# A shorter lead for the weight halves during attention, with attention and the modulation loads moved later

## The chip, the core and the metric

The kernel runs on one core of one Trainium2 chip. The time is the device time of one execution in microseconds (us), as the median of several executions. The profile is one more execution, taken with the hardware profiler; its times within the program are counted from the first instruction ("the span").

TensorE is called PE in the profile (PEld is its loading of weights), VectorE DVE, ScalarE ACT, GpSimd POOL and SyncE SP. SP issues nearly all loads from HBM; its rows are marked SPq.

## The reference

One layer of a transformer variant on 256 tokens of width 1024, in float32: a token mixer with two branches, then a feed-forward part with a short convolution. All of it is modulated by six vectors that come from a condition vector `c`.

```python
mod = silu(c) @ w_ada + b_ada                 # 1024 -> 6 x 1024: sh1, sc1, g1, sh2, sc2, g2
h = x * (1 + sc1) + sh1
proj = h @ w_in                               # 1024 -> mq mk mv (512 each) rq rk (512) rv rg (1024) g_a g_r (1024)
y_a = attention(rope(mq), rope(mk), mv)       # 8 heads of 64, causal (256 tokens make one block)
y_r = retention(rot(rq), rot(rk), rv)         # 4 heads, keys of 128, values of 256, decay mask
y_r = silu(rg) * head_norm(y_r)
merged = sigmoid(g_a) * (y_a @ w_proj_moba) + sigmoid(g_r) * (y_r @ w_proj_ret)
x = layer_norm(ALPHA * x + g1 * (merged @ w_out))
h = x * (1 + sc2) + sh2
g, u = h @ w_ff_gate, h @ w_ff_up             # 1024 -> 2816
y = (gelu(conv3(g)) * u) @ w_ff_down
out = layer_norm(ALPHA * x + g2 * y)
```

## The kernel before

**Products in three parts.** Each float32 operand is split into a high part of a reduced format (`whi`, a copy by ACT) and the rest (`wlo`, a subtraction by DVE: raw minus high). A product is then three matmuls: high by high, high by low, low by high (`mm3`, lines L115 to L117).

**Weight tiles and halves.** Weights come from HBM as raw tiles of 128 x 2048 float32, 1 MB each, into four rotating buffers (`RAW_BUFS = 4`). A raw tile has two halves of 128 x 1024; each half gets one `whi` (line L1261, ACT) and one `wlo` (line L1275, DVE), and eight pairs of these can be alive (`HL_BUFS = 8`). This text numbers weight tiles from 0 at the start of the main stream: tile n holds halves 2n and 2n+1.

**Steps.** After the opening part A (the first modulation vectors, and the first 1024 columns of `w_in` with parts of `g_a`), the program is a list of steps, one for each half. Step s multiplies half s: in the mixer these are 12 matmuls of 128x512. The mixer's steps are, with the two banks of PSUM that they write:

| steps | weights | banks | who reads the banks afterwards |
|---|---|---|---|
| 0 to 3 | rk | 0, 1 | ACT (L485) |
| 4 to 7, 8 to 11 | rv | 2, 3, then 0, 1 | ACT (L493) |
| 12 to 15, 16 to 19 | rg | 2, 3, then 0, 1 | ACT (L501), DVE (L502) |
| 20, 21 and 22, 23 | rest of g_a | 2, 3, then 0, 1 | DVE (L510) |
| 24 to 27, 28 to 31 | g_r | 2, 3, then 0, 1 | ACT (L518) |
| 32, 33 and 34, 35 | w_proj_moba | 2, 3, then 0, 1 | DVE (L525) |
| 36 to 39, 40 to 43 | w_proj_ret | 2, 3, then 0, 1 | DVE (L544) |

A group of steps can't start before the banks it writes have been read out by the engine in the last column, for the group two rows of banks earlier. Steps 44 to 51 are `w_out` and the first layer norm, later ones the feed-forward part.

**What sets the order.** Nothing is rescheduled: each engine executes its instructions in the order in which the program writes them. The loop over the steps writes, for step s: first the side work of two places in the step, and between these the preparation of weight halves (`prep_to`) up to half s plus a lead of `LOOKAHEAD = 6`; then the step's matmuls and what reads out its banks; then the side work of a third place. `prep_halves` writes the high copy of one half further than the subtraction that it is at. So ACT meets the high copy of half s + 7 before the read-out of step s, and whatever that copy waits for, the read-out behind it waits for too.

**Side work** is written as generators that go on at each of the three places. `mixers` is attention: `rope` of the two token halves of q and k (DVE), 16 transposes (`rot_T`, PE line L993), then for 8 heads scores (PE, L1046), the mask with the row maximum (DVE, L1055), the exponential and its scaling (ACT, L1082 and L1078), transposes (PE, L1093) and the product with v (`attend`, PE line L1069). It also ropes rq and rk, and at `i == 10` it starts `retention`, whose first product with the decay mask is DVE line L1157. Its 16 transposes of the result are PE line L1196, and the splits of these are ACT line L92 and DVE line L93.

**Modulation units.** The rest of `w_ada` (sections 2 to 5) comes as units: raw tiles of 1 MB in the same four buffers, placed in the stream of loads behind given weight tiles (`extra`). Each unit is two multiply-and-sum instructions on DVE (line L227, `junk<-raw,srow`, one for each half), of which one is written behind the subtraction of each weight half as long as a unit has arrived. Section 4 is g1, needed at the end of step 47; sections 2 and 3 are needed at the first layer norm.

**Loads.** SP issues the loads in the order of the stream. A load goes into the buffer of the load four places earlier in the stream, and waits in SP's queue until DVE has done with that tile: for a weight tile, the subtraction of its second half; for a unit, its second L227.

Of the kernel before, what the change touches and what calls it, by code (L numbers as in the profile page):

```python
# [17 lines left out]
EPS = 1e-5  # L18
ALPHA = 2.0 ** 0.25
RROPE, RROT, TL = 5, (8, 10), 4  # L20
LOOKAHEAD = 6
RAW_BUFS = 4
HL_BUFS = 8
NG = 4
ROT_AT, RV_AT, RG_AT, LN1_AT = 3, 12, 20, 48


CONST_AT, FIRST = 1, 1
# [32 lines left out]
def _body(nc, a, out, pe, act, dve, sp, cst, wts, big, tmp, ps, dram):  # L61
# [14 lines left out]
    def slot(n, shape, dt=F32):  # L76
        if n in pairs:
            assert pairs[n].dtype == dt
            return pairs[n].rearrange("p e (k t) -> p e k t", k=shape[2])
        if n not in place:  # L80
            return big.tile(shape, dt, tag=f"A{n}", name=f"A{n}")
        pair, e = place[n]
        assert pairs[pair].dtype == dt
        v = pairs[pair][:, e, :math.prod(shape[1:])]
        return v.rearrange("p (a b) -> p a b", a=shape[1]) if len(shape) == 3 else v
# [394 lines left out]
    S = {}  # L480
# [515 lines left out]
                       p.rearrange("p (i t) -> p i t", i=4), AF.Copy)  # L996

    def evac_A():
        v = slot(4, [128, 2, 512])
        for t in range(2):  # L1000
            S["rqk", t] = slot(f"R{t}", [128, 1024])
        for c in range(2):
            for t in range(2):
                o = qk[t][:, c * 512:c * 512 + 512]
                dve.tensor_tensor(o, pa[2 * c + t], o, OP.add)
        for t in range(2):
            act.activation(v[:, t], pa[4 + t], AF.Copy)
        for t in range(2):
            act.activation(S["rqk", t][:, 0:512], pa[6 + t], AF.Copy)
        S["qk"], S["v"] = qk, v  # L1010

    def mixers():

# [4 lines left out]
        roped(0)  # L1018
        for i in range(ROT_AT + 2):
            yield  # L1020
            if i == 0:
                roped(1)
            yield
            if i == ROT_AT + 1:
                for w in range(4):
                    rot_T(qk[w // 2], w // 2, qkT, w % 2, 4 + w)
            yield
# [193 lines left out]


    extra = {}
    for sec, at in ((2, (6, 7, 9, 10)), (3, (11, 12, 13, 14)), (4, (16, 18, 19, 20)), (5, (38, 41, 44, 47))):
        for u in range(4):
            done = (lambda sec=sec: rows_done(sec)) if sec > 3 else (lambda: None)
            extra.setdefault(at[u], []).append((a["ada2"][sec - 2, u], ada_unit(sec, u, done)))
# [61 lines left out]
    def prep_to(n, force=False):  # L1289
        while prepped[0] < min(n, 2 * len(main)) and (force or live[0] < HL_BUFS):  # L1290
            next(pg)
# [6 lines left out]
    pg = prep_halves()  # L1298
    prep_to(FIRST)
    evac_A()  # L1300
    prep_to(FIRST + 2)
    sides = [mixers()]

    def run_sides():
# [4 lines left out]
    for s, (need, rel, fn) in enumerate(steps):  # L1309
        S["main"] = s  # L1310
        if s == LN1_AT + 8:
            sides.append(residual())
        run_sides()
        prep_to(max(need) + 1, True)
        late = LN1_AT < s < LN1_AT + 8
        if not late:
            prep_to(max(need) + 1 + (LOOKAHEAD if s < LN1_AT - 1 else HL_BUFS))
        run_sides()
        for e in waiting:
            if e[0] <= s:  # L1320
                e[1]()
        waiting[:] = [e for e in waiting if e[0] > s]
        fn([tiles[h] for h in need])
        for h in rel:
            tiles.pop(h)
            live[0] -= 1
        while s % 2 and later and later[0][0] <= s:
            later.pop(0)[1]()
        run_sides()
        if late and s >= LN1_AT + PRIME:  # L1330
            if s == LN1_AT + PRIME:
                next(pg)
            elif s > LN1_AT + 4:
                prep_to(max(need) + 1 + HL_BUFS)
# [96 lines left out]
```

## Time and profile before

| what | value |
|---|---|
| median of 3 executions | 426.39 us (426.08 to 426.46) |
| the profiled execution's own time | 427.17 us |
| its span | 425.4 us |
| granted TensorE clock, mean | 0.995 |
| busy: PE / DVE / ACT / POOL | 97% / 87% / 58% / 3% of the span |
| moved by DMA | 105.58 MB, 248 GB/s on average |
| step 0 of the main stream starts on PE | 63.47 us |
| step 18 starts | 129.26 us |
| step 36 starts | 186.68 us |

How to read it: PE's durations are modelled and overlap (a 128x512 matmul is shown with 0.39 us, and the next one starts 0.227 us later), so where PE stood still is read from the starts of its rows. DVE's and ACT's rows overlap a little too; the price of an instruction in a queue is the distance from its start to the next start. In a row of the timeline the first number is the start, the second the duration, and a bracket tells how long the engine was idle before and what ended that.

### The profile page before, as it was taken

What the parts mean: (1) busy time and instruction counts of PE and PEld (TensorE: products, weight loads), DVE (VectorE), ACT (ScalarE), POOL (GpSimd) and SP (SyncE); (2) the same over time, 40 slices, a digit from 0 to 9 for tenths busy, and PEclk for the clock granted to TensorE, in tenths of its full rate; (3) what the DMA queues carried; (4) which work ended last, traced back from release to release, by engine and by line L of the source; (5) the groups of instructions that cost most, each with busy time, mean ns of one, the idle gap of its engine ahead of it and who ended that gap; (6) DMA issues with size and microseconds to landing.
All of it is one profiled execution on the core that took longest, in us unless ns stands there. A gap on an engine that the chain in (4) does not pass through costs nothing.

```text
span 425.4 us, 5803 instructions
## 1 busy us (share of the span) xinstructions
PE 413.5 (97%) x2104; PEld 347.5 (82%) x2104; DVE 370.2 (87%) x613; ACT 245.5 (58%) x397; POOL 14.0 (3%) x26
## 2 busy tenths in 40 slices
PE   7999999999999999999999999999999999999992
PEld 4888887786888888888888898888888888888882
DVE  5979898969998999799777896999999888789876
ACT  4666558759865578524453886655545445455600
POOL 0000000100000000001000001000000010012200
PEclk9999999999999999999999999999999999999997
DMA  8998995886569778689652085985776776540001
GB/s 284 408 410 329 420 416 186 296 346 223 186 277 353 247 296 306 290 324 368 246 197 99 2 309 190 368 300 184 312 245 233 280 282 235 193 186 2 1 25 74
DMA packets 18828, 105.58 MB, mean 248 GB/s; under 512 B 2288, under 2 KB 3568, under 8 KB 8048
## 3 DMA queue, kind: packets, MB, share of 16 engines
q1 hardware_dynamic: 17280, 99.97, 62.7%
q0 software_dynamic: 1376, 4.99, 3.5%
q8 instruction: 16, 0.26, 0.2%
q10 hardware_dynamic: 144, 0.26, 0.2%
q14 instruction: 12, 0.10, 0.1%
HBM read 104.15 MB, written 1.06 MB: 247 GB/s over the span
## 4 chain that ended last, share of the span: by engine, by line
PE 86%; DVE 6%; DMA 3%; ACT 1%; issue 1%; SPq 1%; DVEq 0%; ACTq 0%
PE P L124 16%; PE P L115 14%; PE P L116 14%; PE P L117 14%; PE P L301 13%; PE P L126 8%; DVE wlo L1275 3%; DMA raw<-in_winB 2%; DMA raw<-in_strm 1%; PE P L688 1%; PE P L690 1%; PE P L691 1%; DVE junk L227 1%; PE P L1069 1%; DVE A L1055 1%
## 5 line engine op out<-in xcount | busy, mean ns | idle before, releaser
L1275 DVE TENSOR_TENSOR wlo<-raw,whi 128x1024 fp32r<-128x1024 f32 x118 | 141.9, 1219 | 15.2 <-ACT whi L1261 14.9
L1261 ACT ACTIVATE whi<-raw 128x1024 fp32r<-128x1024 f32 x118 | 122.4, 1057 | 53.8 <-PE P L117 21.0
L115 PE MATMUL P<-whi,AH 128*128 128x512 f32 x160 | 63.5, 397 | 0.6 <-DVE mx L1055 0.6
L116 PE MATMUL P<-wlo,AH 128*128 128x512 f32 x160 | 62.5, 390 | 0.2 <-DVE wlo L1275 0.2
L117 PE MATMUL P<-whi,AH 128*128 128x512 f32 x160 | 62.4, 390 | 0.0
L301 PE MATMUL P<-whi,AH 128*128 128x512 f32 x160 | 42.0, 391 | 1.2 <-DVE AH L267 0.9
L124 PE MATMUL P<-AYa,whi 128*128 128x512 f32 x144 | 39.2, 393 | 0.0
L227 DVE CUSTOM_DVE_ANT_0 junk<-raw,srow 128x1024 bf16<-128x1024 f32 x32 | 38.9, 1217 | 0.0
L124 PE MATMUL P<-AYb,whi 128*128 128x512 f32 x144 | 38.6, 390 | 0.0
L301 PEld LDWEIGHTS P<-whi,AH 128*128 128x128 f32 x160 | 29.8, 188 | 8.8 <-ACT whi L284 2.4
L115 PEld LDWEIGHTS P<-whi,AH 128*128 128x128 f32 x160 | 30.1, 188 | 7.6 <-DVE mx L1055 1.0
L116 PEld LDWEIGHTS P<-wlo,AH 128*128 128x128 f32 x160 | 30.1, 188 | 6.5 <-DVE wlo L1275 0.6
L117 PEld LDWEIGHTS P<-whi,AH 128*128 128x128 f32 x160 | 30.0, 188 | 6.4
L465 ACT ACTIVATE A<-P 128x256 f32<-128x256 f32 x36 | 13.7, 381 | 34.5 <-PE P L126 32.6
L124 PEld LDWEIGHTS P<-AYb,whi 128*128 128x128 f32 x144 | 27.0, 188 | 6.0
L284 ACT ACTIVATE whi<-raw 128x512 fp32r<-128x512 f32 (+1 forms) x26 | 20.8, 824 | 17.8 <-DMA raw<-in_strm 16.6
L287 DVE TENSOR_TENSOR wlo<-raw,whi 128x512 fp32r<-128x512 f32 (+1 forms) x26 | 23.6, 935 | 6.0 <-ACT whi L284 5.9
L124 PEld LDWEIGHTS P<-AYa,whi 128*128 128x128 f32 x144 | 25.1, 190 | 3.6
L126 PEld LDWEIGHTS P<-AYa,wlo 128*128 128x128 f32 x144 | 22.0, 189 | 2.8
L301 PE MATMUL P<-wlo,AH 128*128 128x512 f32 x80 | 23.2, 389 | 0.0
L126 PE MATMUL P<-AYb,wlo 128*128 128x256 f32 x144 | 23.1, 283 | 0.0
L126 PE MATMUL P<-AYa,wlo 128*128 128x256 f32 x144 | 22.9, 282 | 0.0
(302 smaller groups left out, 732.7 us busy)
## 6 DMA issues: line engine op xcount, KB each, us to landing
raw<-in_ada SPq DMA_DIRECT2D x16, 1024.0 KB, 4.9
raw<-in_wup SPq DMA_DIRECT2D x11, 1024.0 KB, 5.5
raw<-in_wgate SPq DMA_DIRECT2D x11, 1024.0 KB, 4.9
raw<-in_wdown SPq DMA_DIRECT2D x11, 1024.0 KB, 5.1
raw<-in_winB SPq DMA_DIRECT2D x10, 1024.0 KB, 7.5
raw<-in_strm SPq DMA_DIRECT2D x8, 1024.0 KB, 7.6
raw<-in_strm SPq DMA_DIRECT2D x12, 512.0 KB, 7.5
raw<-in_winGr SPq DMA_DIRECT2D x4, 1024.0 KB, 6.1
```

The costliest lines, as they stand in the source:

```text
L115: pe.matmul(o, lh, rh, start=start, stop=False)
L116: pe.matmul(o, lh, rl, start=False, stop=False)
L117: pe.matmul(o, ll, rh, start=False, stop=stop)
L124: pe.matmul(o, wh[:, k * 128:(k + 1) * 128], x2[k], start=k == 0, stop=False)
L126: pe.matmul(o[:, :256], wl[:, k * 128:(k + 1) * 128], x2[k][:, 0], start=False, stop=k == n - 1)
L227: dve.tensor_tensor_reduce(out=nobody(j if own else None), in0=raw, in1=srow, scale=1.0, scalar=0.0, op0=OP.mult, op1=OP.add, accum_out=mo ...
L284: act.activation(hi[:, o], raw[:, o], AF.Copy)
L287: dve.tensor_tensor(lo[:, o], raw[:, o], f(hi[:, o]), OP.subtract)
L301: pe.matmul(pa[b0 + c // 512 * 2 + t], x[xi][:, j, t * 128:(t + 1) * 128], ws[k][:, c:c + 512], start=first and (xi, k) == (0, 0), stop=la ...
L465: act.activation(t, p[:, 256:], AF.Copy)
L1261: act.activation(hi, src, AF.Copy)
L1275: dve.tensor_tensor(lo, src, f(hi), OP.subtract)
```

## The change

Five edits.

- While the step is below 22, halves are prepared four ahead of the step and not six (`NEAR`, `NEAR_TO`). From step 22 on it is six as before.
- `evac_A` is cut in two. The four additions on DVE for q and k stay where they were; the four copies on ACT (v, and the first half of rq and rk) become `evac_B`, written behind the preparation of halves 1 to 3; before, they stood ahead of the preparation of halves 1 and 2.
- The rope of the second token half of q and k is written in step 1, not in step 0.
- `ROT_AT` goes from 3 to 4: the transposes of q and k and everything of attention behind them, with the retention that it starts, come one step later.
- The units of sections 2, 3 and 4 move to later places in the stream of loads: section 2 behind weight tiles 9 to 12 (before: 6, 7, 9, 10), section 3 behind 13 to 16 (before: 11 to 14), section 4 behind 17 to 20 (before: 16, 18, 19, 20).

```diff
-LOOKAHEAD = 6
+LOOKAHEAD, NEAR, NEAR_TO = 6, 4, 22
...
-ROT_AT, RV_AT, RG_AT, LN1_AT = 3, 12, 20, 48
+ROT_AT, RV_AT, RG_AT, LN1_AT = 4, 12, 20, 48
...
     def evac_A():
-        v = slot(4, [128, 2, 512])
-        for t in range(2):
-            S["rqk", t] = slot(f"R{t}", [128, 1024])
         for c in range(2):
             for t in range(2):
                 o = qk[t][:, c * 512:c * 512 + 512]
                 dve.tensor_tensor(o, pa[2 * c + t], o, OP.add)
+        S["qk"] = qk
+
+    def evac_B():
+        v = S["v"] = slot(4, [128, 2, 512])
         for t in range(2):
             act.activation(v[:, t], pa[4 + t], AF.Copy)
         for t in range(2):
+            S["rqk", t] = slot(f"R{t}", [128, 1024])
+        for t in range(2):
             act.activation(S["rqk", t][:, 0:512], pa[6 + t], AF.Copy)
-        S["qk"], S["v"] = qk, v
...
         for i in range(ROT_AT + 2):
             yield
-            if i == 0:
+            if i == 1:
                 roped(1)
             yield
             if i == ROT_AT + 1:
...
-    for sec, at in ((2, (6, 7, 9, 10)), (3, (11, 12, 13, 14)), (4, (16, 18, 19, 20)), (5, (38, 41, 44, 47))):
+    for sec, at in ((2, (9, 10, 11, 12)), (3, (13, 14, 15, 16)), (4, (17, 18, 19, 20)), (5, (38, 41, 44, 47))):
...
     prep_to(FIRST)
     evac_A()
-    prep_to(FIRST + 2)
+    prep_to(FIRST + 3)
+    evac_B()
     sides = [mixers()]
...
         if not late:
-            prep_to(max(need) + 1 + (LOOKAHEAD if s < LN1_AT - 1 else HL_BUFS))
+            prep_to(max(need) + 1 + (NEAR if s < NEAR_TO else LOOKAHEAD if s < LN1_AT - 1 else HL_BUFS))
```

**How the instructions move.** First VectorE at the start of the main stream. `wlo` is the subtraction of a weight half, A2a and A2b are the two token halves of q and k, A8a is the rope's scratch tile; the first rows are the additions of `evac_A`. Before:

```order
L1005 TENSOR_TENSOR A2a<-P_132,A2a 128x512
L1005 TENSOR_TENSOR A2b<-P_133,A2b 128x512
L1275 TENSOR_TENSOR wlo<-raw,whi 128x1024 x2
L983 TENSOR_TENSOR A8a<-A2a,tables 128x16x32 x2
L986 TENSOR_TENSOR A2a<-A2a,tables 128x1024
L987 TENSOR_TENSOR A2a<-A2a,A8a 128x1024
L1275 TENSOR_TENSOR wlo<-raw,whi 128x1024 x4
L983 TENSOR_TENSOR A8a<-A2b,tables 128x16x32 x2
L986 TENSOR_TENSOR A2b<-A2b,tables 128x1024
L987 TENSOR_TENSOR A2b<-A2b,A8a 128x1024
L1275 TENSOR_TENSOR wlo<-raw,whi 128x1024 x5
```

Now, the same place:

```order
L1002 TENSOR_TENSOR A2a<-P_132,A2a 128x512
L1002 TENSOR_TENSOR A2b<-P_133,A2b 128x512
L1277 TENSOR_TENSOR wlo<-raw,whi 128x1024 x3
L983 TENSOR_TENSOR A8a<-A2a,tables 128x16x32 x2
L986 TENSOR_TENSOR A2a<-A2a,tables 128x1024
L987 TENSOR_TENSOR A2a<-A2a,A8a 128x1024
L1277 TENSOR_TENSOR wlo<-raw,whi 128x1024 x2
L983 TENSOR_TENSOR A8a<-A2b,tables 128x16x32 x2
L986 TENSOR_TENSOR A2b<-A2b,tables 128x1024
L987 TENSOR_TENSOR A2b<-A2b,A8a 128x1024
L1277 TENSOR_TENSOR wlo<-raw,whi 128x1024 x5
```

Half 3 now stands ahead of the first rope, and two halves stand between the ropes where there were four.

Then SyncE's loads of the main stream: `winB` are weight tiles 0 to 9, `winGa` 10 and 11, `winGr` 12 to 15, `wpm` 16 and 17, `wpr` 18 to 21, and `ada` is a modulation unit. Before, from weight tile 2 on:

```order
L102 DMA raw<-in_winB 128x2048 x5
L102 DMA raw<-in_ada 128x2048
L102 DMA raw<-in_winB 128x2048
L102 DMA raw<-in_ada 128x2048
L102 DMA raw<-in_winB 128x2048 x2
L102 DMA raw<-in_ada 128x2048
L102 DMA raw<-in_winGa 128x2048
```

Now:

```order
L102 DMA raw<-in_winB 128x2048 x8
L102 DMA raw<-in_ada 128x2048
L102 DMA raw<-in_winGa 128x2048
```

Two units have gone from between the weight tiles of the attention steps; they come back further on, one behind weight tile 15 and one behind 17, so that from tile 9 to tile 20 weights and units alternate one by one.

Last, VectorE around halves 32 to 38. `junk` is the multiply-and-sum of a modulation unit, AYa the split of the retention's result, which step 36 multiplies. Before:

```order
L1275 TENSOR_TENSOR wlo<-raw,whi 128x1024 x2
L227 ISA junk,mod<-raw,srow 128x1024
L227 ISA mod 128x1
L1275 TENSOR_TENSOR wlo<-raw,whi 128x1024
L227 ISA junk,mod<-raw,srow 128x1024
L227 ISA mod 128x1
L1275 TENSOR_TENSOR wlo<-raw,whi 128x1024 x3
L227 ISA junk,mod<-raw,srow 128x1024
L227 ISA mod 128x1
L93 TENSOR_TENSOR AYa<-P_1621,AYa 128x4x128
```

Now:

```order
L1277 TENSOR_TENSOR wlo<-raw,whi 128x1024
L227 ISA junk,mod<-raw,srow 128x1024
L227 ISA mod 128x1
L1277 TENSOR_TENSOR wlo<-raw,whi 128x1024
L227 ISA junk,mod<-raw,srow 128x1024
L227 ISA mod 128x1
L1277 TENSOR_TENSOR wlo<-raw,whi 128x1024
L227 ISA junk,mod<-raw,srow 128x1024
L227 ISA mod 128x1
L93 TENSOR_TENSOR AYa<-P_1643,AYa 128x4x128
```

A unit's multiply-and-sum now stands behind every weight half here, where before some halves had none; and the split of the retention's result now stands behind half 38, where it stood behind half 37.

## The prediction

> **What bounds the kernel now.** I first read the span and then TensorE's rows in order of time, looking for places where a matmul starts later than the pitch allows. The profiled execution took 427.17 us in all, 0.78 above the median of 426.39; I work out differences in its span and put them on the median.
>
> ```profile
> span 425.4 us, 5803 instructions
> ```
>
> PE is busy in nearly all of it (97%, in the table above); a change in the order of side work can win only where PE stands still. In the main stream there are four such places, all in steps 3 to 12:
>
> ```profile
> 71.63 0.39 PE L115 MATMUL P<-whi,AH 128*128 128x512 f32 x1
> 72.17 0.50 PE L116 MATMUL P<-wlo,AH 128*128 128x512 f32 x1 [0.15 <-DVE wlo L1275]
> 72.51 0.39 PE L117 MATMUL P<-whi,AH 128*128 128x512 f32 x1
> ...
> 77.63 0.93 PE L993 MATMUL P<-ident,A2a 128*128 128x128 f32 x7
> 79.30 0.55 PE L993 MATMUL P<-ident,A2b 128*128 128x128 f32 x3 [0.75 <-DVE A2b L987]
> ...
> 95.60 1.45 PE L1093 MATMUL P<-ident,A 128*128 128x128 f32 x6
> ...
> 103.84 0.39 PE L117 MATMUL P<-whi,AH 128*128 128x512 f32 x1
> 104.79 0.50 PE L115 MATMUL P<-whi,AH 128*128 128x512 f32 x1 [0.56 <-DVE mx L1055]
> ...
> 118.07 0.82 PE L1093 MATMUL P<-ident,A 128*128 128x128 f32 x6
> ```
>
> Two 128x512 matmuls start 0.227 us apart when nothing stops them. The first stall (half 3's `wlo`, which stands behind the first rope) makes this 0.54, and 0.34 to the next start: 0.42 us. The transposes come at 0.109 us each, so the eight of A2a should have handed over at 78.50 and not 79.30: 0.80 (the second rope is late). Six transposes take 0.82 us undisturbed and took 1.45: 0.63 (scaled exponentials late). Step 12 started 0.95 us after the matmul before it: 0.72 (the mask of heads 6 and 7, which reads the banks that step 12 writes). Sum: 2.57, say **2.6 us**, all there is to win.
>
> Then I read the windows for the engine that would come next.
>
> ```profile
> 90.00:100.00 10.00, 9.80 (x55) 7.54 (x54) 5.93 (x17) 8.66 (x24) 0.00 (x0) 1.00 0.52 186
> 150.00:160.00 10.00, 10.00 (x46) 8.29 (x45) 9.96 (x17) 7.84 (x13) 0.00 (x0) 1.00 0.77 298
> 160.00:170.00 10.00, 10.00 (x46) 8.29 (x45) 10.00 (x15) 8.54 (x13) 0.00 (x0) 1.00 0.89 321
> 180.00:190.00 10.00, 10.00 (x46) 8.29 (x45) 10.00 (x16) 2.77 (x3) 0.00 (x0) 1.00 0.80 288
> ```
>
> The third busy figure is DVE. It is idle 4 us of ten around 95 us, in attention, and full from 150 to 170 and from 180 to 190, with PE never waiting for it there: it lives on the lead that it built up before. The change takes modulation work out of the first stretch and puts it into the second. That is where I look for the price.
>
> **The four stalls, after the change.** The subtractions of halves 1 to 3 now stand ahead of the first rope.
>
> ```profile
> 63.47 0.39 PE L115 MATMUL P<-whi,AH 128*128 128x512 f32 x1
> ...
> 66.03 1.22 DVE L1275 TENSOR_TENSOR wlo<-raw,whi 128x1024 fp32r<-128x1024 f32 x1 [1.41 <-ACT whi L1261]
> 67.18 1.28 DVE L983 TENSOR_TENSOR A8a<-A2a,tables 128x512 f32<-128x512 f32 x2
> ...
> 70.90 4.62 DVE L1275 TENSOR_TENSOR wlo<-raw,whi 128x1024 fp32r<-128x1024 f32 x4
> ...
> 84.85 0.28 DVE L1055 CUSTOM_DVE_ANT_0 A<-P,tables 128x128 f32<-128x128 f32 x1
> 85.59 0.28 DVE L1055 CUSTOM_DVE_ANT_0 A<-P,tables 128x128 f32<-128x128 f32 x1
> ...
> 91.34 1.06 ACT L1261 ACTIVATE whi<-raw 128x1024 fp32r<-128x1024 f32 x1 [4.63 <-DMA raw<-in_winB]
> ```
>
> A rope costs 70.90 - 67.18 = 3.7 us. The wait of 1.41 us goes with `evac_B` behind the high copies, so half 3 is done by about 67, against 71.9 needed; two halves (2.3) and both ropes (7.4) end near 77, and the transposes now stand behind step 5, not before 63.47 + 6 x 2.72 = 79.8. Stalls one and two go. The third goes with the units: in ACT's queue attention's exponentials stood behind the weight copy at 91.34, which waited 4.63 us for its load, and that load came between two unit loads which are now further on. For the fourth, the mask of heads 6 and 7 is written right ahead of step 12, with one step less between. From the second group of scores on, DVE has four masked heads and one subtraction to do, 0.74 (85.59 - 84.85) and 1.14 each, from 0.75 us before step 11 starts, of which the third head must be done when step 12 starts 2.85 later: 3 x 0.75 + 1.14 + 0.1 - 0.75 = 2.74, the 0.1 for a reciprocal. It just fits, if DVE comes to it idle, which it does without units. I take 0; the bounds are 0 and the 0.72 of now. So PE is **2.6 us early at step 18**.
>
> **What the second stretch costs.** Which DVE work must end before PE may go on? Step 36 writes banks 2 and 3, which L525 reads out. So I follow DVE's queue from the retention's first mask product (L1157) to the first half of L525. The product can't come early: it needs PE's scores behind step 18 (17 before).
>
> ```profile
> 128.47 0.38 PE L1155 MATMUL P<-AYa,AYb 128*128 128x128 f32 x2
> 129.26 0.47 PE L115 MATMUL P<-whi,AH 128*128 128x512 f32 x1
> ...
> 127.14 1.22 DVE L1275 TENSOR_TENSOR wlo<-raw,whi 128x1024 fp32r<-128x1024 f32 x1
> 128.28 1.22 DVE L227 CUSTOM_DVE_ANT_0 junk<-raw,srow 128x1024 bf16<-128x1024 f32 x1
> ...
> 129.42 1.02 DVE L1157 TENSOR_TENSOR A<-P,A2a 128x384 f32<-128x384 f32 x2
> ...
> 135.55 1.21 DVE L1157 TENSOR_TENSOR A<-P,A2b 128x384 f32<-128x384 f32 x2 [1.65 <-PE P L1155]
> ...
> 175.95 1.29 DVE L93 TENSOR_TENSOR AYa<-P,AYa 128x512 fp32r<-128x512 f32 x2 [2.87 <-ACT AYa L92]
> ...
> 182.91 1.28 DVE L525 TENSOR_TENSOR A<-P,A 128x512 f32<-128x512 f32 x2
> ```
>
> Before: from 129.42 to the end of L525's first half, 182.91 + 0.6 = 183.5, are 54.1 us, of which 1.65 and 2.87 idle: 49.6 us of work. In it are 16 subtractions (halves 24 to 39) and 12 unit halves (9 to 20, from 0). Now DVE arrives at L1157 with only half 22 and four unit halves behind it, so the same stretch holds 17 subtractions (23 to 39) and 17 unit halves (4 to 20). Each costs 1.14 us (127.14, 128.28, 129.42): 6 x 1.14 = 6.8 us more, **56.4 us**.
>
> The start: PE's scores of the first head were done at 128.47 + 0.38 = 128.85, 0.4 before the next step began (129.26). That next step, now 19, begins at 129.26 + 2.72 - 2.6 = 129.4, so L1157 can start at 129.0. DVE stands idle before it, about 3 us, because the lead of four keeps all later halves behind it in the queue. Add waits for the second head (0.2) and for the second product, whose scores end 6.3 us into step 19 (135.6; DVE is there at about 134.8): 1.0 in all. L525's first half ends at 129.0 + 56.4 + 1.0 = **186.4**, with no wait for a load.
>
> Loads come next. With units and weights alternating, weight tile 18 goes into tile 16's buffer, free after half 33, and tile 19 into tile 17's, free after half 35.
>
> ```profile
> 168.56 0.33 SPq L102 DMA_DIRECT2D raw<-in_wpr  x1
> 180.74 0.33 SPq L102 DMA_DIRECT2D raw<-in_ada  x1
> 181.88 0.33 SPq L102 DMA_DIRECT2D raw<-in_wpr  x1
> ...
> raw<-in_wpr SPq DMA_DIRECT2D x1, 1024.0 KB, 4.7
> raw<-in_ada SPq DMA_DIRECT2D x1, 1024.0 KB, 4.8
> raw<-in_wpr SPq DMA_DIRECT2D x1, 1024.0 KB, 6.3
> raw<-in_winGr SPq DMA_DIRECT2D x1, 1024.0 KB, 6.8
> ...
> 173.40 1.06 ACT L1261 ACTIVATE whi<-raw 128x1024 fp32r<-128x1024 f32 x1 [3.50 <-DMA raw<-in_wpr]
> 174.36 1.07 ACT L518 ACTIVATE A<-P 128x512 f32<-128x512 f32 x2
> ```
>
> The first three landing times are of the three issues above, in their order (the fourth is of an issue at 128.39): 4.7 us alone, and of two issued 1.14 apart 4.8 and 6.3, so the second lands 2.65 after the first. Tile 18 is asked for some 1.9 us after a unit: it lands 4.8 + 2.65 - 1.9 = 5.5 after its issue. With 0.1 to issue, 0.1 to ACT and 1.06 for the high copy, half 36 can start 6.8 us after half 33 ended; in the queue stand five instructions, 5.8 us: 1.0 late. Tile 19 is asked for 1.2 after a unit: 6.25, in all 7.5, against five instructions and that 1.0, 6.7: 0.8 late. L525's first half ends at 186.4 + 1.8 = **188.2**.
>
> ```profile
> 181.24 0.39 PE L115 MATMUL P<-whi,A 128*128 128x512 f32 x1
> 186.68 0.39 PE L115 MATMUL P<-whi,AYa 128*128 128x512 f32 x1
> ```
>
> Steps 34 and 36 started here; unhindered they would now start at 178.6 and 184.1. The first waits as well: it writes banks that ACT reads out with L518, and in ACT's queue L518 stands behind the high copy of half 38, that of tile 19. Counting back from 188.2 (the rest of L525, half 39, a unit half, four L93 of 0.6, a unit half, half 38) that copy ends at 180.6, the first L518 half a microsecond later, and step 34 starts at 181.2, 2.6 late. Step 36 then waits 1.7 more, until 188.3. Removed 2.6, new 4.3: **1.6 us later than 186.68**. Behind it nothing waits: by the same count half 37 is subtracted over 10 us before step 37, and DVE had idle time there before, too. 427.17 becomes 428.8, and the median **428.0**.
>
> Bounds of that term: if both loads land in 4.7, step 36 starts at 186.5 (-0.2); if in 6.8, the longest in this stretch, each adds about 0.5 (+2.6). The mask at step 12, at its worst 0.7, delays L1157 by as much.
>
> [...]
>
> **The rivals.**
> - *DVE alone decides, loads are in time.* For it: tile loads often land in 4.7. Against: from tile 9 on each weight load follows a unit load closely. Step 36 at 186.5: 426.2, no change.
> - *The stalls go and nothing comes back.* One mechanism: DVE keeps enough lead, so that L525 is read out before 184.1. For it: in the windows from 150 us on PE is busy throughout. It decides if the stretch from L1157 to L525 takes under 55 us instead of 59.2; I see no row for that. 426.39 - 2.6 = 423.8, the other side.
> - *Loads land later than reckoned* (over 6.8 in a row, with the 186 to 321 GB/s of the windows growing towards 400), or the mask stalls step 12: 429.2.
>
> **How the numbers follow.** Forecast 0.56, the rivals 0.20, 0.12 and 0.12. About 0.2% (0.85 us) is what a measurement of this kernel tells from no change: under 425.54 is faster, over 427.24 slower. Faster: the second rival and a trace of the first, 0.13. Same: the first and the low end of the forecast, 0.08: 0.27. Slower: 0.60. Range: 425.9 to 429.2, which leaves out the second rival and a little above.
>
> **What would show it.** Right: no stall in steps 3 to 12; DVE idle about 3 us ahead of L1157; L518 of g_r's second half behind a high copy that waited for a load; a stall of over 2 us at step 34 and one at step 36, released by ACT and by DVE; step 36 at about 188. Wrong: L525 starting before 185, or the high copy of half 38 not waiting for its load. If PE still stalls in steps 3 to 12, the first sum failed; if step 36 starts on time, the second.

## The result, and the profile after

The changed kernel takes **432.25 us** (median of 4 executions, 431.65 to 432.49) against 426.42 (426.08 to 426.74): a ratio of **1.0135**, 95% interval 1.0117 to 1.0152. It is slower by 5.8 us; forecast were 1.6 us, and 432.25 lies above the range.

In the page of the profile the share of each engine says little: PE 416.4 us of 429.9.

```profile
span 429.9 us, 5794 instructions
PE 416.4 (97%) x2104; PEld 349.6 (81%) x2104; DVE 370.8 (86%) x613; ACT 246.0 (57%) x397; POOL 14.0 (3%) x26
```

The span grew by 4.5 us, the profiled execution's own time from 427.17 to 431.65. The rest, up to the 5.8 of the medians, is spread between executions: 431.65 is the shortest of the change's four, and 427.17 is above the median of before.

From about L1020 on, lines stand two further down in the changed file: L1275 is now L1277, L1261 is L1263, L1157 is L1159. First the place of the old stalls, on PE in the changed kernel (the timeline; the number in front is the start):

```profile
79.88 1.03 PE L993 MATMUL P<-ident,A2a 128*128 128x128 f32 x8
80.75 1.04 PE L993 MATMUL P<-ident,A2b 128*128 128x128 f32 x8
...
96.97 0.82 PE L1095 MATMUL P<-ident,A 128*128 128x128 f32 x6
```

The second eight transposes now follow the first at 0.87 us, which is 8 x 0.109, and the six of attention take 0.82: the stalls of 0.80 and 0.63 are gone. So are the other two; between 60 and 170 us no matmul starts over 0.2 us later than the pitch allows. Step 19 starts at 129.20, where 129.4 was forecast: PE is early by what was said.

Then steps 34 and 36, in the same view:

```profile
183.41 0.80 PE L115 MATMUL P<-whi,A 128*128 128x512 f32 x1 [4.33 <-ACT A L518]
184.00 0.63 PE L116 MATMUL P<-wlo,A 128*128 128x512 f32 x1
184.43 0.63 PE L117 MATMUL P<-whi,A 128*128 128x512 f32 x1
...
188.23 0.39 PE L117 MATMUL P<-whi,A 128*128 128x512 f32 x1
```

Step 34 starts at 183.41, 4.5 us late (its last matmul before, at 178.69, needed 0.23), and waits for ACT, as forecast. What was not forecast stands in the rows behind it: the matmuls now start 0.43 us apart instead of 0.227, for eleven of them. The windows show why, in the third figure from the end, the granted clock (the two behind it are the DMA engines' busy share and GB/s):

```profile
170.00:180.00 10.00, 8.93 (x47) 6.95 (x45) 8.43 (x14) 4.93 (x8) 0.00 (x0) 1.00 0.95 382
183.40:188.40 5.00, 4.99 (x12) 3.97 (x13) 4.96 (x8) 4.36 (x8) 0.00 (x0) 0.52 1.01 387
```

PE had been idle for 4.3 us, and its clock stood at 0.52 in the window behind that. Step 36 starts at 191.18, 4.5 us behind the 186.68 of before: that is the whole difference in span. On ACT and on DVE:

```profile
176.41 2.01 ACT L1263 ACTIVATE whi<-raw 128x1024 fp32r<-128x1024 f32 x2 [3.48 <-PE P L1198]
181.81 1.06 ACT L1263 ACTIVATE whi<-raw 128x1024 fp32r<-128x1024 f32 x1 [3.40 <-DMA raw<-in_wpr]
182.78 1.07 ACT L518 ACTIVATE A<-P 128x512 f32<-128x512 f32 x2
```

```profile
128.83 1.21 DVE L1159 TENSOR_TENSOR A<-P,A2a 128x384 f32<-128x384 f32 x2 [3.32 <-PE P L1157]
...
155.47 1.23 DVE L227 CUSTOM_DVE_ANT_0 junk<-raw,srow 128x1024 bf16<-128x1024 f32 x1 [0.55 <-DMA raw<-in_ada]
159.27 1.23 DVE L1277 TENSOR_TENSOR wlo<-raw,whi 128x1024 fp32r<-128x1024 f32 x1 [0.57 <-ACT whi L1263]
162.69 1.23 DVE L1277 TENSOR_TENSOR wlo<-raw,whi 128x1024 fp32r<-128x1024 f32 x1 [0.25 <-ACT whi L1263]
177.50 1.23 DVE L1277 TENSOR_TENSOR wlo<-raw,whi 128x1024 fp32r<-128x1024 f32 x1 [1.53 <-ACT whi L1263]
182.90 1.23 DVE L1277 TENSOR_TENSOR wlo<-raw,whi 128x1024 fp32r<-128x1024 f32 x1 [0.76 <-ACT whi L1263]
...
189.99 1.28 DVE L525 TENSOR_TENSOR A<-P,A 128x512 f32<-128x512 f32 x2
```

L518 stands behind the high copy of half 38 (181.81), and that waited 3.4 us for its load. The copy at 176.41 is put down to PE's transposes, whose result it does not read; its tile was asked for at 170.09, needed 6.2 us and landed at about 176.30. On DVE every bracket behind the first of these rows comes from a load: at 155.47 directly, at 159.27, 177.50 and 182.90 through the high copy. The 0.25 at 162.69 is one step further: that half lies in the same tile as the one before, but its copy stood in ACT's queue behind a sigmoid (L511), and this behind the copy that had waited. Together they are 0.55 + 0.57 + 0.25 + 1.53 + 0.76 = 3.7 us, where the prediction had 1.8. The first half of L525, on which step 36 depends, ends at 190.67 (the pair starts at 189.99, one takes 0.68).

How the four loads that were asked for between 148 and 156 us landed (the last column is us from issue to landing):

```profile
raw<-in_ada SPq DMA_DIRECT2D x1, 1024.0 KB, 6.4
raw<-in_winGr SPq DMA_DIRECT2D x1, 1024.0 KB, 7.8
raw<-in_ada SPq DMA_DIRECT2D x1, 1024.0 KB, 6.8
raw<-in_wpm SPq DMA_DIRECT2D x1, 1024.0 KB, 8.1
```

The prediction's rows of before had 4.7 alone, 4.8 and 6.3 for two, and one of 6.8.

### The profile page after: what moved, and what is told of

It is laid out like the page before. It is cut to its first block, busy times and chain, and to the rows that moved or that the text cites. A ratio compares the mean times of both kernels' runs of the same rounds, so it can differ in the third digit from the quotient of the medians.

```text
span 429.9 us, 5794 instructions
## 1 busy us (share of the span) xinstructions
PE 416.4 (97%) x2104; PEld 349.6 (81%) x2104; DVE 370.8 (86%) x613; ACT 246.0 (57%) x397; POOL 14.0 (3%) x26
## 4 chain that ended last, share of the span: by engine, by line
PE 87%; DVE 8%; DMA 3%; issue 1%; ACT 0%; DVEq 0%; ACTq 0%; SPq 0%
PE P L124 15%; PE P L115 14%; PE P L116 14%; PE P L117 14%; PE P L301 13%; PE P L126 8%; DVE junk L227 2%; DVE wlo L1277 2%; DMA raw<-in_wpm 2%; DMA raw<-in_wpr 2%; PE P L688 1%; PE P L690 1%; PE P L691 1%; PE P L993 1%; PE P L1048 1%
## 5 line engine op out<-in xcount | busy, mean ns | idle before, releaser
L1277 DVE TENSOR_TENSOR wlo<-raw,whi 128x1024 fp32r<-128x1024 f32 x118 | 142.0, 1218 | 17.0 <-ACT whi L1263 17.0
L1263 ACT ACTIVATE whi<-raw 128x1024 fp32r<-128x1024 f32 x118 | 122.0, 1055 | 48.5 <-PE P L117 14.4
```

Of the source, the lines that this page charges most:

```text
L1263: act.activation(hi, src, AF.Copy)
L1277: dve.tensor_tensor(lo, src, f(hi), OP.subtract)
```

## The experiments

The table shows all runs, with what their traces have at the place that matters. "Queue" is the number of subtractions plus unit halves on DVE between the first L1157 and the first L525; then come the end of L525's first half and the starts of steps 34 and 36. Each ratio stands against runs of the kernel before on the same chip (medians 426.3 to 426.8).

| kernel | time, us | ratio (95%) | queue | L525 | step 34 | step 36 |
|---|---|---|---|---|---|---|
| before | 426.42 | | 16+12 | 183.6 | 181.2 | 186.7 |
| the change | 432.25 | 1.0135 (1.0117 to 1.0152) | 17+17 | 190.7 | 183.4 | 191.2 |
| units back | 426.88 | 1.0005 (0.9993 to 1.0018) | 17+13 | 186.2 | 180.2 | 186.3 |
| lead 6 | 426.58 | 1.0000 (0.9988 to 1.0012) | 15+15 | 185.4 | 178.3 | 185.5 |
| read-out first | 433.89 | 1.0169 (1.0149 to 1.0189) | 17+17 | 190.8 | 178.6 | 191.0 |
| PE kept busy | 432.14 | 1.0130 (1.0102 to 1.0159) | 17+17 | 190.7 | 183.4 | 190.9 |
| units alone | 431.86 | 1.0113 (1.0083 to 1.0144) | 16+16 | 190.7 | 182.1 | 190.9 |
| moves alone | 428.74 | 1.0048 (1.0028 to 1.0068) | 15+11 | 185.5 | 183.4 | 188.8 |
| no unit loads | 428.38 | 1.0029 (1.0014 to 1.0043) | 17+17 | 186.5 | 178.5 | 186.7 |
| unit loads of 128 KB | 427.81 | 1.0033 (1.0022 to 1.0044) | 17+17 | 187.6 | 180.3 | 187.7 |
| of 256 KB | 428.36 | 1.0051 (1.0036 to 1.0066) | 17+17 | 187.3 | 179.9 | 187.5 |
| of 512 KB | 432.19 | 1.0109 (1.0067 to 1.0150) | 17+17 | 190.7 | 183.4 | 191.7 |
| loads in two pieces | 431.13 | 1.0108 (1.0077 to 1.0139) | 17+17 | 190.6 | 183.3 | 190.7 |
| section 3 late, lead 4 | 428.00 | 1.0029 (1.0018 to 1.0041) | 17+12 | 184.2 | 180.0 | 185.5 |
| section 3 late, lead 6 | 424.79 | 0.9953 (0.9936 to 0.9969) | 15+10 | 179.5 | 178.1 | 183.6 |
| the same again | 424.84 | 0.9964 (0.9951 to 0.9978) | 15+10 | 179.5 | 178.5 | 183.9 |
| before, section 3 late | 426.46 | 0.9994 (0.9980 to 1.0007) | 16+11 | 182.5 | 179.7 | 185.1 |

### Which part of the change costs

The changed kernel with the units at their old places:

```diff
-    for sec, at in ((2, (9, 10, 11, 12)), (3, (13, 14, 15, 16)), (4, (17, 18, 19, 20)), (5, (38, 41, 44, 47))):
+    for sec, at in ((2, (6, 7, 9, 10)), (3, (11, 12, 13, 14)), (4, (16, 18, 19, 20)), (5, (38, 41, 44, 47))):
```

> The changed kernel with the modulation units at their places of before (sections 2, 3 and 4 behind weight tiles 6, 7, 9, 10; 11 to 14; 16, 18, 19, 20); the lead of four and all moves of attention stay. Theory U (the late units take the time: they fill VectorE and the load buffers between steps 18 and 36): no stall at step 34, the high copy of half 38 ends before 176, and the time is 423.8 to 425.5. Theory L (the short lead takes it): step 34 still waits over 2 us, the time is over 429.

With the lead of six:

```diff
-LOOKAHEAD, NEAR, NEAR_TO = 6, 4, 22
+LOOKAHEAD, NEAR, NEAR_TO = 6, 6, 22
```

> The changed kernel with the lead of six halves in all steps; the late units and the moves of attention stay. Theory U: the units are as late as in the change, so most of the loss stays, 427.5 to 432. Theory L: the stall at step 34 is gone, 424 to 425.5. Theory U and L together (either alone would have been carried by the other's slack): between, 425.5 to 427.5.

Both are back at the time of before. The first missed theory U's band by 1.4 us: step 36 still waits 0.7 us for L525, and step 12 waits 1.4 us for its mask. The second lies where U and L were both needed for the loss. Then the kernel before with the units alone at the new places (the first diff, turned round):

> The kernel before with one part of the change alone: the modulation units of sections 2 to 4 at their new, later places; lead of six, old copies, old order of ropes and attention. Theory D (the loss needs the late units together with the lead of four, and the place where it is paid is step 36, which waits for the vector engine's read-out): with a lead of six no wait of over 2 us at step 34; step 36 waits some 1 to 2 us and starts within 0.7 us of the 186.7 of the kernel before, since the stall at the exponentials (0.6 us) goes and the queue ahead of the read-out is longer; the time is within 0.2 percent of before. Rival U (the later units alone are the loss): 429 us or more.

And the changed kernel with both diffs, which leaves the copies, the ropes and the later attention:

> The change without its two costly parts: the lead of six throughout and the units at their old places, so that only the second rope, the joined transposes, the copies and the later attention are left. Theory D (a short queue ahead of the read-out, since the vector engine comes to the retention with more halves done): no wait at step 34, under 0.8 us at step 36; the stalls at half 3 and the second rope are gone (1.2 us), and one of 0.7 to 1.4 us ahead of step 12 is left, as with the lead of four and the old units: 425.0 to 426.5 us. Rival S (with the lead of six, the subtractions stand ahead of attention again and the stalls return): 426.5 us or more.

The units alone cost 5.1 us, and here rival U was right: the loss does not need the lead of four. The moves alone cost 2.45; D had the gain right at half 3 and at the rope, and missed the size of one stall, at step 12:

```profile
102.44 0.39 PE L117 MATMUL P<-whi,AH 128*128 128x512 f32 x1
105.31 0.50 PE L115 MATMUL P<-whi,AH 128*128 128x512 f32 x1 [2.49 <-DVE mx L1057]
...
106.17 0.63 PE L115 MATMUL P<-whi,AH 128*128 128x512 f32 x1
```

With attention one step later, the masks that step 12 waits for (L1055 before, L1057 here) stand behind subtractions and unit halves, and PE stops for 2.65 us instead of 0.72, with half the clock for 3.4 us behind it (0.68, 0.50 and 0.96 in the three windows of 2 us from 105.3 to 111.3). Not every execution shows that loss: the two with a mean clock of 0.994 and 0.995 took 426.67 and 427.24, the four with 0.990 and 0.991 took 428.41 to 429.36. So the parts are not to be added up: the later units clear the masks, and the moves leave DVE less to do between the retention and L525. In the lead-6 run 15 subtractions and 15 unit halves are left in the queue, and in the run of the units alone 16 and 16 with more waits for loads; step 36 starts at 185.5 in the one, at 190.9 in the other.

### What step 36 waits for

No look-ahead preparation in steps 27 and 31, so that L518 stands ahead of the high copies:

```diff
-        if not late:
+        if not late and s not in (27, 31):
```

> The changed kernel, but in steps 27 and 31 no halves are prepared ahead, so that ScalarE reads out g_r's banks (L518) ahead of the high copies of halves 35 and 38. If ScalarE's order alone is the cost: step 34 starts at 178.7 and the time is about 424. If VectorE is late as well, as the prediction had it: step 34 starts on time, but step 36 then waits for L525 until 188 or later, 427.5 to 430, with a clock dip if that wait is over 4 us.

Eighteen matmuls with a tile of zeros behind step 33, in the group of banks that is complete then, so that PE has work until step 34 may start:

```diff
...
+            if c == 0:
+                for i in range(18):
+                    pe.matmul(bk[1], zr, hh[:, 2 * (i % 4):2 * (i % 4) + 2].rearrange("p a b -> p (a b)"), start=False, stop=i == 17)
...
```

> The changed kernel with 18 more matmuls of 128x512 behind step 33, which add products with a tile of zeros to a finished bank, so that TensorE works 4.1 of the 4.7 us in which it waited ahead of step 34. Nothing else moves. If the lower clock in step 34 (starts 0.427 apart, not 0.227) came from that idle time, step 34 runs at 0.227 and the time falls by 2.0 to 2.4 us, to about 430. If something else slowed step 34, the time stays at 432.2 or above.

In the first, step 34 starts on time, at 178.61, and step 36 still waits:

```profile
190.95 0.77 PE L115 MATMUL P<-whi,AYa 128*128 128x512 f32 x1 [6.59 <-DVE A L525]
```

In the second the zeros fill the gap and step 34 starts at full clock (1.00 from 183.4 to 188.4 us, where the change had 0.52; its matmuls are back at 0.39 us from 0.63), to no gain (L528 is L525 here, three lines further down):

```profile
179.22 4.38 PE L525 MATMUL P<-AH,zr 128*128 128x512 f32 x18
183.44 0.50 PE L115 MATMUL P<-whi,A 128*128 128x512 f32 x1
183.78 0.39 PE L116 MATMUL P<-wlo,A 128*128 128x512 f32 x1
...
190.85 0.47 PE L115 MATMUL P<-whi,AYa 128*128 128x512 f32 x1 [1.68 <-DVE A L528]
```

Whatever happens at step 34, L525 sets step 36, at 190.9. The wait at step 34 and the half clock lie beside that queue in the changed kernel; of these two runs it is the first that pays for the clock, in step 36 itself (0.50 from 190.9 to 193 us), and it is the slowest of all. Its expectation of a lower clock behind a wait of over 4 us was an estimate of the author's, for which there was only the change's wait of 4.3 us; the wait here was 6.6 us, and three shorter than 4 us cost the clock as well (last section). Both expectations were too low: the first still held the prediction's 188 for step 36, and the second did not reckon with L525 behind step 34.

### DVE's own work, or the loads

The unit halves keep their places and multiply the weight half that was just split; the twelve loads are left out:

```diff
         stream.append((src, None))
-        stream += extra.get(i, [])
+        for un in extra.get(i, []):
+            if i < 21:
+                stream[-1] = (src, (un[1],))
+            else:
+                stream.append(un)
...
```

> The changed kernel, but the units of sections 2 to 4 do their multiplications on the weight half that was just split, at the same places of the vector engine's queue, and their twelve loads of 1 MB are left out: so the modulation of those sections is of other numbers, and the twelve tiles of the modulation's weight are not read. It tells the load waits from the vector engine's own work. Theory D (of the 4.5 us that step 36 lost, what goes beyond the engine's own work is waits for loads): the first half of the read-out ends at about 186.4 us as the prediction's sum without load waits has it, step 34 does not wait over 1 us, step 36 starts at 186 to 187, and the time is 426 to 427.5 us. Rival W (the vector engine's work itself is longer than 56.4 us, loads matter little): step 36 not before 188.5, 428.5 us or more.

The queue is the same, and it no longer waits. The groups of DVE between L1159 and L525 (behind the bar: busy us, mean ns, idle time before them and what ended it), first of the changed kernel, then of this one:

```profile
L227 DVE CUSTOM_DVE_ANT_0 junk<-raw,srow 128x1024 bf16<-128x1024 f32 x17 | 20.7, 1217 | 0.5 <-DMA raw<-in_ada 0.5
L1277 DVE TENSOR_TENSOR wlo<-raw,whi 128x1024 fp32r<-128x1024 f32 x17 | 20.6, 1214 | 3.1 <-ACT whi L1263 3.1
```

```profile
L227 DVE CUSTOM_DVE_ANT_0 junk<-raw,srow 128x1024 bf16<-128x1024 f32 x17 | 20.7, 1217 | 0.0
L1283 DVE TENSOR_TENSOR wlo<-raw,whi 128x1024 fp32r<-128x1024 f32 x17 | 20.6, 1213 | 0.0
```

And step 36 of this kernel on PE:

```profile
186.65 0.47 PE L115 MATMUL P<-whi,AYa 128*128 128x512 f32 x1 [2.52 <-DVE A L525]
```

Theory D held in the trace: the queue ends at 186.50 without loads, and the loads are worth 190.67 - 186.50 = **4.2 us**. The median, 428.38, is 0.9 above the expected band, while the profiled execution took 427.11 and its span is that of before. The mean granted clock tells the ten executions apart: the three with 0.996 took 426.9 to 427.2, as expected, the seven with 0.990 to 0.992 took 428.1 to 428.9. In the traced one, of the first kind, step 36 starts 2.7 us late at full clock (1.00 from 186.6 to 192.6 us); that the others lost their clock at this wait is likely, but not traced.

### Why the loads are late

A unit's load does two things: it moves 1 MB, and it holds one of four buffers. With the buffers and the instructions as they are, each unit load brought half, a quarter or an eighth of its tile (the half is shown; the others load and multiply 512 and 256 columns):

```diff
...
+            if fn and fn.secs < 5:
+                t = raw_tile()
+                sp.dma_start(t[:, 0:1024], src[:, 0:1024])
+                loaded.append((t, fn))
...
```

> The changed kernel, but each of the twelve loads for the units of sections 2 to 4 brings only half a tile (512 KB), and the unit's second half multiplies the first half of the tile again: the same instructions of the vector engine in the same places, the same number of loads and buffers, six of the stretch's 24 MB less; the modulation of those sections leaves out half of its weight. It asks why the loads were late. Theory B (bytes: with a unit load behind every weight load the queue is almost full, 0.86 to 0.95 of the sixteen engines between 150 and 190 us): the share there falls to some 0.7, the read-out's first half ends at 186.5 to 187.5 us, step 34 does not wait over 1 us, step 36 starts by 187.7. Rival R (the time until a buffer is free and the landing of a load by itself): the read-out ends no earlier than 189, step 36 starts at 189.5 or later, 430 us or more.

> As the run with half unit loads, but each of the twelve brings 128 KB (256 of 2048 columns), which the unit's two halves multiply four times over: same instructions on the vector engine, same buffers in the same order, 10.5 of the stretch's 24 MB less; the modulation of those sections leaves out seven eighths of its weight. Half the bytes changed nothing, so theory H (a unit's tile holds one of the four buffers until its two halves are multiplied, so that a weight tile is asked for late, whatever the bytes): the read-out's first half ends at 188.5 us or later and step 36 starts after it, 429 us or more. Rival B (bytes, with a threshold that half tiles did not reach): the read-out ends at 186.4 to 187.3, as without unit loads, and 427 to 428.5 us.

> As the run with small unit loads, but each of the twelve brings 256 KB (512 of 2048 columns), which the unit's two halves multiply twice over; the modulation of those sections leaves out three quarters of its weight. Between 128 KB (read-out done at 187.56) and 512 KB (190.66, as with the full 1024 KB) something changes. Theory B (bytes delay the weight tiles in proportion until the queue has no gap left): between the two, 188 to 189.5, and 428 to 430.5 us. Rival X (only the very small loads help, since then the weight tile's load has the queue to itself from the start): 190 or later, and 431 us or more.

How the loads landed that were asked for between 148 and 176 us, of the changed kernel, then with 512 and 256 KB:

```profile
raw<-in_ada SPq DMA_DIRECT2D x5, 1024.0 KB, 5.3
raw<-in_wpm SPq DMA_DIRECT2D x2, 1024.0 KB, 6.6
raw<-in_wpr SPq DMA_DIRECT2D x2, 1024.0 KB, 6.5
raw<-in_winGr SPq DMA_DIRECT2D x1, 1024.0 KB, 7.8
```

```profile
raw<-in_ada SPq DMA_DIRECT2D x5, 512.0 KB, 3.5
raw<-in_wpm SPq DMA_DIRECT2D x2, 1024.0 KB, 6.5
raw<-in_wpr SPq DMA_DIRECT2D x2, 1024.0 KB, 6.3
raw<-in_winGr SPq DMA_DIRECT2D x1, 1024.0 KB, 6.3
```

```profile
raw<-in_wpm SPq DMA_DIRECT2D x2, 1024.0 KB, 5.8
raw<-in_wpr SPq DMA_DIRECT2D x2, 1024.0 KB, 5.1
raw<-in_ada SPq DMA_DIRECT2D x5, 256.0 KB, 3.0
raw<-in_winGr SPq DMA_DIRECT2D x1, 1024.0 KB, 6.2
```

With half units the read-out ends at the same 190.7, but by another wait. The two weight tiles of the foursome (the loads asked for between 148 and 156 us) land sooner, after 6.3 and 6.7 us and not 7.8 and 8.1, and DVE no longer waits at 155, 159 and 163 us. What is left is almost all one wait, for tile 19 (lines stand further down here):

```profile
raw<-in_wpr SPq DMA_DIRECT2D x1, 1024.0 KB, 7.3
...
182.89 1.23 DVE L1283 TENSOR_TENSOR wlo<-raw,whi 128x1024 fp32r<-128x1024 f32 x1 [2.65 <-ACT whi L1269]
```

That tile was asked for at about 174.4 and landed at about 181.7, as in the changed kernel (174.85, after 6.9 us). With a quarter and with an eighth it needs 4.8 us, and the read-out ends at 187.3 and 187.6. One of the four executions with half units took only 428.71, near the 428.36 of the quarter; the other three, 432.16 to 432.68, are at the changed kernel's time. So R's numbers came out for the half in three executions of four, H fell with the eighth, and neither the proportion nor X describes the quarter.

Without unit loads the read-out ended at 186.5. So with the buffers held as in the change, the buffers and what is left of the bytes are worth about 1 us of the 4.2 (187.3 and 187.6 against 186.5), and the bytes that were left out 3.1 to 3.3. Why these come back between 256 and 512 KB, in most executions and not in all, is open; with one trace for each size, a threshold and a single late tile can't be told apart. The DMA engines' mean busy share between 150 and 190 us has no such step: 0.92 (whole), 0.75 (half), 0.66 (quarter), 0.62 (eighth).

Each tile of the stream by two loads of 512 KB, first half first:

```diff
-            loaded.append((load_raw(src), fn))
+            loaded.append((load_raw(src, 2), fn))
```

> The changed kernel, with each 1 MB tile of the stream loaded by two loads of 512 KB, first half first, so that the first half's copy need not wait for the second. Theory H with its other half (the vector engine waits because a load is asked late and lands 5 to 8 us later): the first halves land some 1.3 us sooner (half of the 2.65 us that a tile takes), three to four such waits lie ahead of the read-out, it ends 1.5 to 3 us earlier, at 187.5 to 189.2, and the time is 429 to 431 us. Rival N (the landing is set by the queue's other loads, or twice as many loads cost what they save): the read-out within 0.7 us of 190.7, 431.5 us or more.

The read-out ends at 190.56, as rival N has it; the time, 431.13, lies between the two bands. The two loads of tile 19 are issued in a row, from 175.07 on, and need

```profile
raw<-in_wpr SPq DMA_DIRECT2D x2, 512.0 KB, 6.9
```

6.9 us in the mean, where the whole tile needed 6.9: the first half came 6.5 us after its issue. Here, with others in flight, cutting the load did not bring its first half forward by the 1.3 us that were expected.

### Fewer units ahead of step 36

If queue and loads ahead of step 36 are the price, both shrink when a section moves behind it:

```diff
-    for sec, at in ((2, (9, 10, 11, 12)), (3, (13, 14, 15, 16)), (4, (17, 18, 19, 20)), (5, (38, 41, 44, 47))):
+    for sec, at in ((4, (9, 10, 11, 12)), (2, (13, 14, 15, 16)), (3, (21, 22, 23, 24)), (5, (38, 41, 44, 47))):
```

> The changed kernel with the same twelve units in another order: section 4 in the first four places, section 2 in the next four, and section 3 behind weight tiles 21 to 24, so that eight unit halves (8 x 1.14 = 9.1 us of the vector engine) and four loads leave the stretch ahead of step 36 and stand behind it. Theory D: neither step 34 nor step 36 waits, step 36 starts at about 184.1 us, and if the stretch from step 36 to step 48 has room for them, the time is 423.8 to 424.6 us. Rival G (the work is given back in steps 37 to 48, where the vector engine was also nearly full): 426 us or more, with a stall between steps 37 and 48.

> The same order of units as in the run before it, with a lead of six halves throughout. Theory D: the 1.75 us that step 36 waited with the lead of six and the changed units goes, and nothing else: 424.4 - 1.75 = 422.7 us of span, 423.9 to 424.9 us of time; the two leads then differ by less than 0.5 us. Rival G: 426 us or more.

> The fastest kernel so far once more, in more rounds and beside the moves alone: 424.3 to 425.3 us, a ratio of 0.995 to 0.997 to the kernel before.

> The kernel before with the order of units that was fastest (section 4, section 2, then section 3 behind weight tiles 21 to 24), and nothing else of the change: it tells whether the other edits of the change are worth something once the units no longer stand ahead of step 36. Theory D: the stalls at half 3 and at the second rope (0.42 + 0.80 us) stay, the one at the exponentials goes, and step 36 does not wait: 0.6 to 1.4 us under before, 425.0 to 426.2 us, and 1.2 us or more behind the changed kernel with that order and a lead of six. Rival U (without the other edits the vector engine comes some 4 us later to the retention, as in the run with the units alone, and step 36 still waits): 427 us or more.

With the lead of six, no matmul from 60 us on starts over 0.31 us later than the pitch allows, and 15 subtractions and 10 unit halves stand in the queue:

```profile
L1277 DVE TENSOR_TENSOR wlo<-raw,whi 128x1024 fp32r<-128x1024 f32 x15 | 18.0, 1214 | 1.2 <-ACT whi L1263 1.2
L227 DVE CUSTOM_DVE_ANT_0 junk<-raw,srow 128x1024 bf16<-128x1024 f32 x10 | 12.2, 1219 | 0.0
```

Step 36 starts without a wait,

```profile
183.58 0.39 PE L115 MATMUL P<-whi,AYa 128*128 128x512 f32 x1
```

3.1 us earlier than before, and this kernel beats that before by 0.36 and 0.47% in two comparisons, and so the changed one, too. With the lead of four there is no gain, against D: on PE, step 32 waits for ACT's read-out of g_r, which stands behind a high copy that waited 1.9 us for its load, and two more stops, 0.9 and 0.5 us beyond the pitch, come at 212 and 216 us, of the kind that G named:

```profile
172.66 0.50 PE L115 MATMUL P<-whi,A 128*128 128x512 f32 x1 [1.50 <-ACT A L518]
...
212.33 0.63 PE L536 MATMUL P<-ident,A 128*128 128x128 f32 x4 [0.70 <-DVE A L545]
216.46 0.50 PE L117 MATMUL P<-whi,AH 128*128 128x512 f32 x1 [0.31 <-DVE AH L93]
```

The same order of units in the kernel before gains nothing that can be measured (426.46, just above D's band): the stalls at half 3 and the rope stay. So the change's other edits are worth 1.1 to 1.6 us (each kernel against before on its own chip), once the units are out of the way and the lead stays at six.

## Why the prediction was right or wrong

**The four stalls: right.** All went, the mask at step 12 included. L1159 started at 128.83, forecast 129.0, after 3.3 us of waiting for PE, forecast 3. That the mask costs nothing depended on the units, as was written; with the units back it stops PE for 1.4 us (units back) and 2.65 (moves alone).

**DVE's queue: right.** 17 subtractions and 17 unit halves were counted and are there, and without unit loads L525's first half ends at 186.50; the sum said 186.4. That it fits to 0.1 is partly luck: the work is 56.8 us and not 56.4, the waits ahead of it 0.8 and not 1.0, the start 128.9 and not 129.0.

**The loads: the step that failed.** "1.0 late" and "0.8 late" for weight tiles 18 and 19, together 1.8 us, measured as 4.2 (190.67 - 186.50). The brackets on DVE add up to 3.7; counted from start to start, as the prediction counts, the same five waits are 4.1. For tile 19 the wait was right (0.76), for tile 18 it was 1.53, 0.5 more than said. The larger part was left out: the sum began with tile 18 and took every load before it as in time, while at 155, 159 and 163 us DVE waited 0.55, 0.57 and 0.25 because of the foursome, whose loads needed 6.4 to 8.1 us. The landing times were taken from before, where the rows used had two loads together and no such foursome, and a unit behind every weight tile from 9 to 20 was counted as DVE work but not as loads for all of them. The upper end of the range used 6.8 us for both loads, "the longest in this stretch"; it was a row of another arrangement. By the prediction's own count it also gives about +2.2 and not +2.6, since a later tile 18 leaves less to wait for at tile 19; both are far under the 4.5 that came.

**Step 34: the mechanism right, the size not.** L518 stood behind half 38's copy, as said; that copy ended at 182.87 and not 180.6, and the wait was 4.5 us and not 2.6. **Step 36** was to wait another 1.7 for L525. In its place came the half clock (0.52 from 183.4 to 188.4 us): step 34's matmuls took so long that step 35 ended when L525 was done. The run that keeps PE busy shows that step 36 would otherwise have waited 1.8 us; it starts there at 190.85 and in the change at 191.18, so by estimate the clock itself cost about 0.3 us.

**The rivals.** "Loads later than reckoned" was the right direction at 0.12, with 429.2 too little. "DVE alone" is what the run without unit loads shows: step 36 at 186.65, forecast 186.5. "Nothing comes back" exists too, at 424.8, but only with section 3's eight unit halves behind step 36 and a lead of six.

**The rate.** The rival of later loads had the windows' GB/s growing towards 400. In the changed kernel the window from 170 to 180 us has 382 GB/s, and that from 183.4 to 188.4 us has 387. But a rate alone would not tell why, with half the bytes, tile 19 still needed 7.3 us: there the windows from 170 to 180 and from 180 to 190 us have 274 and 207 GB/s.

## What to carry over

Where side work is moved to a later stretch, count its loads there as well as its instructions: here a load that landed in 4.7 us alone took 5.1 to 8.1 when every weight tile had another load beside it, and one row from a looser stretch is no bound. Follow the queue to the read-out that a later step needs, and test it with the loads left out: that separates work from waiting in one run. Parts of a change can each cost and together cost nothing, or the reverse; here the useful version kept three of the five edits and moved the units further.

## What the runs showed of the hardware

TensorE's granted clock stood at half at the end of some of its waits or behind them. In the change, behind a wait of 4.5 us, it was 0.50 for 6.8 us (181.3 to 188.2). With unit loads of 512 KB, behind 4.3 us, the window from 180 to 190 us has 0.66, which is half clock for 6.8 us as well; with the read-out first, behind 6.8 us, it was 0.50 from 190.9 to 193 us and 0.53 from there to 195. Behind waits of 3.5 us (loads in two pieces), 3.2 us (units alone, step 36) and 2.65 us (moves alone) the windows add up to 3.4 us of half clock each. In the change it began 2.1 us before PE went on, with the units alone 1.1 us after. Behind waits of 1.4 us (units back, step 12), 2.0 us (units alone, step 34) and 2.05 us (unit loads of 256 KB, step 36) it was 1.00, and so it was behind 2.68 us without unit loads, a little more than the 2.65 of the moves alone. No run shows what decides this.

A weight tile that landed in 4.7 us alone (before, asked for at 168.56) took, when asked for between 148 and 176 us, 5.1 to 8.1 us beside unit loads of 1 MB, and 4.8 to 6.8 us beside those of 256 KB. Beside those of 512 KB it took 5.4 to 7.3 us, and the time was that of 1 MB in three executions of four. No run shows the cause.
